# Heads in pairs: products on one half of the partitions next to those on the other half, in attention and in the stick-breaking mixer

## The chip, the cores and the metric

The kernel runs on 1 core of one Trainium2 chip. The metric is the device time of one execution in microseconds (us), as the median of several runs.

## The reference

The program is two transformer blocks in a row, on 256 positions of width 1024, all in float32. The change touches one mixer of each block. In the first block this is sliding-window attention with 16 query heads of 64 and 2 key heads, a window of 128 and a learned sink, for each block of 128 queries against its own and the previous 128 keys:

```
s = einsum('bqhgd,bkhd->bhgqk', qj, kj) * 64 ** -0.5        # where(band), else -inf
m = maximum(max(s, axis=-1), sink)
p = exp(s - m);  denom = sum(p, axis=-1) + exp(sink - m)
out = einsum('bhgqk,bkhd->bqhgd', p / denom, vj)
```

In the second block it is stick-breaking attention with 8 heads of 64, strictly causal (s < t), in two blocks of 128 queries:

```
z = einsum('bhtd,bhsd->bhts', q, k) * scale
sp = where(causal, softplus(z), 0);  rest = cumsum(sp, reverse=True) - sp
w = where(causal, exp(log_sigmoid(z) - rest), 0)
out = einsum('bhts,bhsd->bhtd', w, v)
```

Around them stand, in the first block, an mLSTM mixer, gates and output products and a PEER layer (a gather of 16 experts for each of 8 heads and each position); in the second block an HGRN2 mixer, gates, output products and a gated feed-forward layer.

## The kernel before, in words

The activations lie transposed (features on the partitions) as pairs of a high and a low float32r tile; the projections take three matmuls for each pair (L123, L126, L127). Their weights are streamed from memory in tiles of 128x1024 (`stream`, L112), copied by ScalarE (hi) and subtracted by VectorE or GpSimd (lo, L110).

The order in which each engine's instructions stand is not that of the source: a planner takes them by their place in the source and by when they would be ready in its own model of time. So projections that come later in the source fill the waits of the heads. `after(later, earlier)` (L96) ties two instructions in that order without a semaphore. In the second block the pieces of the mixers are laid between the projections by `weave` (L174) at the places `W_SB`, `W_HG` and so on (L28 to L31).

PSUM has eight banks: four of the tag "acc" (projections), two of "sm" and two of "s".

Attention (L473 to L519) runs over two blocks of queries (`tt`), two key heads (`g`) and two halves (`par_`). The transposed queries `qT` hold two heads in each 128 partitions, the even one on the partitions 0 to 63 and the odd one on 64 to 127, and `kT` holds each key head twice, on both halves. One unit of the loop (`tt`, `g`, `par_`) does four heads of one half: a mask is written into a bank of the tag "sm" by a matmul over all 128 partitions (L487), the scores of two or four heads are added to it by matmuls over 64 partitions (L491), VectorE takes the maximum (L494) and ScalarE the exponential (L499) into `pt_`, which has three buffers under the tag "s4"; then the sum and the sink (L502 to L505), the product with the reciprocal (L506), four transposes into a bank of the tag "s" (L510), a copy by ScalarE for the first block of keys and by VectorE for the second (L513, L515), and the product with the values, 64 columns of weights, into one half of the partitions of the bank `po` (L516). A group (`tt`, `g`) ends with the split of `po` into `attTh` and `attTl` (shown as aTh, aTl), which `mix_a` (L653, matmuls L123 to L127) reads.

Stick-breaking: `sb_z` (L940) writes for each of four heads a mask (L948) and the scores (L949, L950) into an "sm" bank, copies it (L951) and takes the minimum (L952); `sb_out` (L978) multiplies the weights with the values (L986, L987), two heads into the two halves of the partitions of one bank.

A float32 matmul is recorded in the profile as two MATMULs, each with its own load of weights.

Of the kernel before, what the change touches and what calls it, by code (L numbers as in the profile page):

```python
# [16 lines left out]
AF = mybir.ActivationFunctionType  # L17
ALU = mybir.AluOpType
# [29 lines left out]
def peer_hybrid_kernel(ctx: ExitStack, tc: tile.TileContext, A: dict, out: bass.AP, dbg=None, stop=None):  # L48
# [277 lines left out]
    with ExitStack() as c1:  # L326
# [146 lines left out]
        for tt in range(2):  # L473
            for g in range(2):
                po = bank("s")
                for par_ in range(2):
                    heads = [g * 8 + par_ + 2 * i for i in range(4)]
                    hs = slice(g * 8 + par_, g * 8 + par_ + 7, 2)
                    pr = slice(par_ * 64, par_ * 64 + 64)
                    W = P * (tt + 1)  # L480
                    per = 512 // W
                    pt_ = ten([P, 4, W], "pP", bufs=3, tag="s4")
                    nm = ten([P, 4], "nm", bufs=2)
                    sums = ten([P, 4], "sums", bufs=2)
                    for i0 in range(0, 4, per):
                        b = bank()
                        T.matmul(b, identb, (m_gt4.rearrange("p a b -> p (a b)") if tt == 0 else  # L487
                                             m_band.rearrange("p a c b -> p (a c b)")), start=True, stop=False)
                        for i in range(i0, i0 + per):
                            h = heads[i]  # L490
                            T.matmul(b[:, (i - i0) * W:(i - i0 + 1) * W], qT[pr, h // 2, tt * P:(tt + 1) * P],  # L491
                                     kT[pr, g, 0:W], start=False, stop=i == i0 + per - 1)
                        bv = b.rearrange("p (i s) -> p i s", i=per)
# [4 lines left out]
                        for i in range(i0, i0 + per):  # L498
                            S.activation(pt_[:, i], bv[:, i - i0], AF.Exp, bias=nm[:, i:i + 1],  # L499
                                         accum_out=sums[:, i:i + 1])  # L500
                    es = ten([P, 4], "es", bufs=2)
                    V.tensor_tensor(es, nm, par("sink")[:, hs], op=ALU.add)  # L502
                    S.activation(es, es, AF.Exp)
                    V.tensor_tensor(es, es, sums, op=ALU.add)
                    V.reciprocal(es, es)  # L505
                    V.tensor_tensor(pt_, pt_, bc(es.unsqueeze(2), [P, 4, W]), op=ALU.mult)  # L506
                    for sb in range(tt + 1):
                        b = bank("s")
                        for i in range(4):
                            T.transpose(b[:, i * P:(i + 1) * P], pt_[:, i, sb * P:(sb + 1) * P], ident)  # L510
                        pT = ten([P, 512], "pT", bufs=2)
                        if sb == 0:
                            S.activation(pT, b, AF.Copy)  # L513
                        else:
                            V.tensor_copy(pT, b)  # L515
                        T.matmul(po[pr, :], kv[:, sb, P + g * 64:P + g * 64 + 64], pT, start=sb == 0, stop=sb == tt)  # L516
# [319 lines left out]
    with ExitStack() as c4:  # L836
# [103 lines left out]
        def sb_z(g):  # L940
            zc = ten([P, 4, 384], "zc", bufs=2)
            l_ = ten([P, 4, 384], "sl", bufs=2)
            for i in range(4):
                h = g * 4 + i
                m, pr = h // 2, slice(h % 2 * 64, h % 2 * 64 + 64)
                z = bank()
                zz = z[:, 0:384]
                T.matmul(zz, identb, m_sb.rearrange("p a b -> p (a b)"), start=True, stop=False)  # L948
                T.matmul(z[:, 0:256], kT2[pr, m, 0:P], qT2[pr, m, :], start=False, stop=False)  # L949
                T.matmul(z[:, 256:384], kT2[pr, m, P:256], qT2[pr, m, P:256], start=False, stop=True)  # L950
                S.activation(zc[:, i], zz, AF.Copy)  # L951
                V.scalar_tensor_tensor(l_[:, i], zz, -1.0, zc[:, i], op0=ALU.mult, op1=ALU.min)  # L952
# [25 lines left out]
        def sb_out(g):  # L978
            zc = sb[g]["zc"]
            for m in range(g * 2, g * 2 + 2):  # L980
                ob = bank("s")
                for u in range(2):
                    h = m * 2 + u
# [252 lines left out]
```

## Time and profile before

| what | value |
|---|---|
| runs of the kernel | 1372.96, 1373.87, 1379.27 us; median 1373.87 |
| the profiled execution, its own time | 1372.99 us |
| its span, first to last instruction | 1371.2 us |
| busy: PE, DVE, ACT, POOL | 1202.5, 894.8, 514.4, 565.6 us |
| mean granted clock of TensorE | 0.951 |
| read from memory | 381.42 MB, 279 GB/s over the span |

The table is read so: PE is TensorE's matmuls, PEld its loads of weights, DVE VectorE, ACT ScalarE, POOL GpSimd. A busy share is a mean over stages of different kinds; the stages are, in order, the first block's mixers (to about 330 us), the gather of the experts (to about 960 us), and the second block.

### The profile page before, as it was taken

The page shows a single profiled execution, that of the slowest core. Times are in us where ns is not written, and L with a number is a line of the kernel's source. Part 1 is how long each engine was busy: PE and PEld are TensorE (multiplying, and loading weights), DVE is VectorE, ACT ScalarE, POOL GpSimd, SP SyncE. Part 2 cuts the span into 40 slices and gives each one's busy share as a digit, 9 for nine tenths or more (in the row PEclk, how much of TensorE's full clock was granted, in tenths as well). Part 3 has the DMA queues.
Part 4 walks back from the last instruction along what each step waited for, and adds up shares of the span by engine and source line. Part 5 has one row for each costly group of instructions (what it writes and reads, how often), then busy time and mean ns, then how long its engine had stood idle before and what let it go on. Part 6 is the DMA issues. An engine that isn't in the chain of part 4 may idle for free.

```text
span 1371.2 us, 16704 instructions
## 1 busy us (share of the span) xinstructions
PE 1202.5 (88%) x5785; PEld 832.8 (61%) x5785; DVE 894.8 (65%) x1963; ACT 514.4 (38%) x927; POOL 565.6 (41%) x394
## 2 busy tenths in 40 slices
PE   8999999994977778788877777887999999999998
PEld 7976789983333333333323333332788999899987
DVE  6966658558577776667877666765589786543521
ACT  6565434453122222212322221221475464544442
POOL 4311412542444435354444544443100005488874
PEclk9999999995899989899999999999999999999999
DMA  7533335666999999999999999999355335556554
GB/s 220 171 136 108 124 93 164 196 195 247 426 427 427 427 427 425 427 427 413 419 424 422 427 415 421 418 423 428 114 169 170 108 95 185 182 164 203 184 197 144
DMA packets 69779, 383.56 MB, mean 280 GB/s; under 512 B 8000, under 2 KB 8512, under 8 KB 36928
## 3 DMA queue, kind: packets, MB, share of 16 engines
q0 software_dynamic: 36864, 268.45, 46.7%
q1 hardware_dynamic: 31968, 112.15, 25.9%
q10 hardware_dynamic: 864, 1.90, 0.4%
q8 instruction: 46, 0.75, 0.2%
q14 instruction: 37, 0.30, 0.1%
HBM read 381.42 MB, written 1.05 MB: 279 GB/s over the span
## 4 chain that ended last, share of the span: by engine, by line
PE 44%; DMA 29%; DVE 17%; issue 4%; POOL 4%; ACT 1%; POOLq 0%; DVEq 0%; SPq 0%; ACTq 0%
DMA ga<-in_peer_du_dram,idx 28%; PE acc L123 10%; PE acc L126 10%; PE acc L127 10%; DVE jk L796 6%; POOL ga L793 3%; PE acc L805 2%; PE sm L126 1%; PE sm L123 1%; PE sm L127 1%; POOL lo L110 1%; PE sm L491 1%; DVE lo L110 1%; PE sm L1055 1%; PE s L516 1%
## 5 line engine op out<-in xcount | busy, mean ns | idle before, releaser
L805 PE MATMUL acc<-ga,dg 128*128 128x512 f32 x1024 | 497.9, 645 | 149.6 <-ACT dg L802 149.6
L805 PEld LDWEIGHTS acc<-ga,dg 128*128 128x128 f32 x1024 | 206.9, 207 | 439.5 <-issue 242.7
L793 POOL DMA_INDIRECT ga<-in_peer_du_dram,idx x256 | 292.1, 1141 | 356.0 <-PE acc L805 207.1
L796 DVE SCALAR_TENSOR_TENSOR jk<-ga,xn 128x1024 bf16<-128x1024 f32 x256 | 313.3, 1224 | 191.3 <-DMA ga<-in_peer_du_dram,idx 190.9
L110 POOL TENSOR_TENSOR lo<-raw,hi 128x1024 fp32r<-128x1024 f32 (+1 forms) x88 | 218.3, 2486 | 375.8 <-PE acc L127 243.6
L106 ACT ACTIVATE hi<-raw 128x1024 fp32r<-128x1024 f32 (+1 forms) x210 | 220.5, 1052 | 252.2 <-PE acc L127 54.6
L110 DVE TENSOR_TENSOR lo<-raw,hi 128x1024 fp32r<-128x1024 f32 (+1 forms) x122 | 163.1, 1338 | 94.0 <-ACT hi L106 36.2
L123 PE MATMUL acc<-T1l,hi 128*128 128x256 f32 x384 | 108.4, 283 | 0.3 <-DVE T1l L239 0.3
L126 PE MATMUL acc<-T1h,lo 128*128 128x256 f32 x384 | 108.4, 282 | 0.0
L127 PE MATMUL acc<-T1h,hi 128*128 128x256 f32 x384 | 107.8, 281 | 0.0
L123 PE MATMUL acc<-lo,T1h 128*128 128x512 f32 (+1 forms) x256 | 99.7, 395 | 2.2 <-DVE lo L110 2.0
L126 PE MATMUL acc<-hi,T1l 128*128 128x512 f32 (+1 forms) x256 | 100.2, 392 | 0.7 <-DVE T1l L308 0.6
L127 PE MATMUL acc<-hi,T1h 128*128 128x512 f32 (+1 forms) x256 | 99.9, 391 | 0.0
L123 PEld LDWEIGHTS acc<-T1l,hi 128*128 128x128 f32 x384 | 72.5, 189 | 1.9 <-issue 0.7
L127 PEld LDWEIGHTS acc<-T1h,hi 128*128 128x128 f32 x384 | 72.3, 188 | 0.9 <-issue 0.4
L126 PEld LDWEIGHTS acc<-T1h,lo 128*128 128x128 f32 x384 | 72.2, 188 | 1.0 <-issue 0.5
L126 PEld LDWEIGHTS acc<-hi,T1l 128*128 128x128 f32 x256 | 49.3, 192 | 12.0 <-DVE T1l L308 2.0
L123 PEld LDWEIGHTS acc<-lo,T1h 128*128 128x128 f32 x256 | 48.7, 192 | 11.5 <-DVE lo L110 2.2
L127 PEld LDWEIGHTS acc<-hi,T1h 128*128 128x128 f32 x256 | 49.1, 192 | 10.3 <-issue 1.0
L126 PE MATMUL sm<-fhTh,lo 128*128 128x256 f32 x176 | 48.5, 277 | 0.0
L127 PE MATMUL sm<-fhTh,hi 128*128 128x256 f32 x176 | 48.4, 276 | 0.0
L126 PE MATMUL acc<-fhTh,lo 128*128 128x256 f32 x176 | 48.4, 277 | 0.0
(849 smaller groups left out, 1984.2 us busy)
## 6 DMA issues: line engine op xcount, KB each, us to landing
raw<-in_w_in_dram SPq DMA_DIRECT2D x92, 512.0 KB, 3.5
raw<-in_w_fg_dram SPq DMA_DIRECT2D x22, 512.0 KB, 3.6
raw<-in_w_fu_dram SPq DMA_DIRECT2D x22, 512.0 KB, 3.8
raw<-in_w_fd_dram SPq DMA_DIRECT2D x22, 512.0 KB, 4.2
raw<-in_w_out_dram SPq DMA_DIRECT2D x16, 512.0 KB, 3.6
raw<-in_w_ba_dram SPq DMA_DIRECT2D x8, 512.0 KB, 3.5
raw<-in_w_bm_dram SPq DMA_DIRECT2D x8, 512.0 KB, 4.0
raw<-in_peer_wq_dram SPq DMA_DIRECT2D x8, 512.0 KB, 4.2
```

Of the source, the lines that this page charges most:

```text
L106: S.activation(dst_h, src, AF.Copy)
L110: return (V if eng == "v" else G).tensor_tensor(dst_l, src, dst_h.bitcast(F32), op=ALU.subtract)
L123: m = T.matmul(o, lh, rl, start=start, stop=False)
L126: T.matmul(o, ll, rh, start=False, stop=False)
L127: return T.matmul(o, lh, rh, start=False, stop=stop)
L491: T.matmul(b[:, (i - i0) * W:(i - i0 + 1) * W], qT[pr, h // 2, tt * P:(tt + 1) * P], kT[pr, g, 0:W], start=False, stop=i == i0 + per - 1)
L516: T.matmul(po[pr, :], kv[:, sb, P + g * 64:P + g * 64 + 64], pT, start=sb == 0, stop=sb == tt)
L793: G.indirect_dma_start(ga, None, A["peer_du"], bass.IndirectOffsetOnAxis(idx[tt][h][:, r0 + j:r0 + j + 1], 0))
L796: dot = V.scalar_tensor_tensor(jk, ga[:, 0:D], 1.0, xn[:, tt], op0=ALU.mult, op1=ALU.mult, accum_out=s_[:, j:j + 1])
L805: T.matmul(uacc[tt][dh], dg[:, j], rows[j][:, D + dh * 512:D + dh * 512 + 512], start=h + r0 + j == 0, stop=h == 7 and r0 + j == 15)
L1055: T.matmul(b[:, tt * 4 + m], xl_[:, m, tt], xr_[:, m, tt, :, 1], start=tt + m == 0, stop=tt + m == 4)
```

## The change

Attention: the two halves `par_` of a group are worked on together. For each group there are two score tiles, two sets of maxima and sums (four buffers each). The masks of both halves are written first, into the two "sm" banks; then the score matmuls of the halves alternate, head by head, and all are tied behind the second mask. The maxima and exponentials follow for the one half and then the other, and the sums, reciprocals and products likewise. For each block of keys both halves are transposed and copied, the first half's copy by ScalarE and the second's by VectorE (`pT` has three buffers), and then the two products with the values follow each other, the second half's first, tied behind the last transpose and to one another.

Stick-breaking: `sb_z` takes two heads at a time, with both masks first and the score matmuls alternating; `sb_out` alternates the products of its two heads.

```diff
@@ -473,47 +473,61 @@
         for tt in range(2):
             for g in range(2):
                 po = bank("s")
-                for par_ in range(2):
-                    heads = [g * 8 + par_ + 2 * i for i in range(4)]
-                    hs = slice(g * 8 + par_, g * 8 + par_ + 7, 2)
-                    pr = slice(par_ * 64, par_ * 64 + 64)
-                    W = P * (tt + 1)
-                    per = 512 // W
-                    pt_ = ten([P, 4, W], "pP", bufs=3, tag="s4")
-                    nm = ten([P, 4], "nm", bufs=2)
-                    sums = ten([P, 4], "sums", bufs=2)
-                    for i0 in range(0, 4, per):
-                        b = bank()
-                        T.matmul(b, identb, (m_gt4.rearrange("p a b -> p (a b)") if tt == 0 else
+                W = P * (tt + 1)
+                per = 512 // W
+
+
+                two_ = (0, 1)
+                pts = [ten([P, 4, W], "pP", bufs=3, tag="s4") for _ in two_]
+                nms = [ten([P, 4], "nm", bufs=4) for _ in two_]
+                sms = [ten([P, 4], "sums", bufs=4) for _ in two_]
+                for i0 in range(0, 4, per):
+                    bs = [bank() for _ in two_]
+                    for b in bs:
+                        mk = T.matmul(b, identb, (m_gt4.rearrange("p a b -> p (a b)") if tt == 0 else
                                              m_band.rearrange("p a c b -> p (a c b)")), start=True, stop=False)
-                        for i in range(i0, i0 + per):
-                            h = heads[i]
-                            T.matmul(b[:, (i - i0) * W:(i - i0 + 1) * W], qT[pr, h // 2, tt * P:(tt + 1) * P],
-                                     kT[pr, g, 0:W], start=False, stop=i == i0 + per - 1)
-                        bv = b.rearrange("p (i s) -> p i s", i=per)
+                    for i in range(i0, i0 + per):
+                        for par_ in two_:
+                            h = g * 8 + par_ + 2 * i
+                            pr = slice(par_ * 64, par_ * 64 + 64)
+                            after(T.matmul(bs[par_][:, (i - i0) * W:(i - i0 + 1) * W],
+                                           qT[pr, h // 2, tt * P:(tt + 1) * P], kT[pr, g, 0:W], start=False,
+                                           stop=i == i0 + per - 1), mk)
+                    for par_ in two_:
+                        nm = nms[par_]
+                        bv = bs[par_].rearrange("p (i s) -> p i s", i=per)
                         V.tensor_reduce(nm[:, i0:i0 + per], bv, axis=AX.X, op=ALU.max)
                         hsi = slice(g * 8 + par_ + 2 * i0, g * 8 + par_ + 2 * (i0 + per) - 1, 2)
                         V.scalar_tensor_tensor(nm[:, i0:i0 + per], nm[:, i0:i0 + per], -1.0, nsink[:, hsi],
                                                op0=ALU.mult, op1=ALU.min)
                         for i in range(i0, i0 + per):
-                            S.activation(pt_[:, i], bv[:, i - i0], AF.Exp, bias=nm[:, i:i + 1],
-                                         accum_out=sums[:, i:i + 1])
+                            S.activation(pts[par_][:, i], bv[:, i - i0], AF.Exp, bias=nm[:, i:i + 1],
+                                         accum_out=sms[par_][:, i:i + 1])
+                for par_ in two_:
+                    hs = slice(g * 8 + par_, g * 8 + par_ + 7, 2)
                     es = ten([P, 4], "es", bufs=2)
-                    V.tensor_tensor(es, nm, par("sink")[:, hs], op=ALU.add)
+                    V.tensor_tensor(es, nms[par_], par("sink")[:, hs], op=ALU.add)
                     S.activation(es, es, AF.Exp)
-                    V.tensor_tensor(es, es, sums, op=ALU.add)
+                    V.tensor_tensor(es, es, sms[par_], op=ALU.add)
                     V.reciprocal(es, es)
-                    V.tensor_tensor(pt_, pt_, bc(es.unsqueeze(2), [P, 4, W]), op=ALU.mult)
-                    for sb in range(tt + 1):
+                    V.tensor_tensor(pts[par_], pts[par_], bc(es.unsqueeze(2), [P, 4, W]), op=ALU.mult)
+                for sb in range(tt + 1):
+                    pTs = []
+                    for par_ in two_:
                         b = bank("s")
                         for i in range(4):
-                            T.transpose(b[:, i * P:(i + 1) * P], pt_[:, i, sb * P:(sb + 1) * P], ident)
-                        pT = ten([P, 512], "pT", bufs=2)
-                        if sb == 0:
+                            tr = T.transpose(b[:, i * P:(i + 1) * P], pts[par_][:, i, sb * P:(sb + 1) * P], ident)
+                        pT = ten([P, 512], "pT", bufs=3)
+                        if par_ == 0:
                             S.activation(pT, b, AF.Copy)
                         else:
                             V.tensor_copy(pT, b)
-                        T.matmul(po[pr, :], kv[:, sb, P + g * 64:P + g * 64 + 64], pT, start=sb == 0, stop=sb == tt)
+                        pTs.append(pT)
+                    for par_ in (1, 0):
+                        pv = T.matmul(po[par_ * 64:par_ * 64 + 64, :], kv[:, sb, P + g * 64:P + g * 64 + 64],
+                                      pTs[par_], start=sb == 0, stop=sb == tt)
+                        after(pv, tr)
+                        tr = pv
                 pv = po.rearrange("p (k t) -> p k t", k=4)
                 split(attTh[:, g * 4:g * 4 + 4, tt * P:(tt + 1) * P], attTl[:, g * 4:g * 4 + 4, tt * P:(tt + 1) * P],
                       pv, "v")
@@ -940,16 +954,19 @@
         def sb_z(g):
             zc = ten([P, 4, 384], "zc", bufs=2)
             l_ = ten([P, 4, 384], "sl", bufs=2)
-            for i in range(4):
-                h = g * 4 + i
-                m, pr = h // 2, slice(h % 2 * 64, h % 2 * 64 + 64)
-                z = bank()
-                zz = z[:, 0:384]
-                T.matmul(zz, identb, m_sb.rearrange("p a b -> p (a b)"), start=True, stop=False)
-                T.matmul(z[:, 0:256], kT2[pr, m, 0:P], qT2[pr, m, :], start=False, stop=False)
-                T.matmul(z[:, 256:384], kT2[pr, m, P:256], qT2[pr, m, P:256], start=False, stop=True)
-                S.activation(zc[:, i], zz, AF.Copy)
-                V.scalar_tensor_tensor(l_[:, i], zz, -1.0, zc[:, i], op0=ALU.mult, op1=ALU.min)
+            for i in range(0, 4, 2):
+                m = (g * 4 + i) // 2
+                zs = [bank()[:, 0:384] for _ in range(2)]
+                for zz in zs:
+                    mk = T.matmul(zz, identb, m_sb.rearrange("p a b -> p (a b)"), start=True, stop=False)
+                for s0 in range(2):
+                    for u, zz in enumerate(zs):
+                        pr = slice(u * 64, u * 64 + 64)
+                        after(T.matmul(zz[:, s0 * 256:384 if s0 else 256], kT2[pr, m, s0 * P:s0 * P + P],
+                                       qT2[pr, m, s0 * P:], start=False, stop=s0 == 1), mk)
+                for u, zz in enumerate(zs):
+                    S.activation(zc[:, i + u], zz, AF.Copy)
+                    V.scalar_tensor_tensor(l_[:, i + u], zz, -1.0, zc[:, i + u], op0=ALU.mult, op1=ALU.min)
             S.activation(l_, l_, AF.Exp)
             sb[g].update(zc=zc, l=l_)
 
@@ -979,12 +996,13 @@
             zc = sb[g]["zc"]
             for m in range(g * 2, g * 2 + 2):
                 ob = bank("s")
-                for u in range(2):
-                    h = m * 2 + u
-                    pr = slice(u * 64, u * 64 + 64)
-                    w_ = zc[:, h % 4]
-                    T.matmul(ob[pr, 0:256], vs[:, 0, h * 64:(h + 1) * 64], w_[:, 0:256], start=True, stop=False)
-                    T.matmul(ob[pr, P:256], vs[:, 1, h * 64:(h + 1) * 64], w_[:, 256:384], start=False, stop=True)
+                for s0 in range(2):
+                    for u in range(2):
+                        h = m * 2 + u
+                        pr = slice(u * 64, u * 64 + 64)
+                        w_ = zc[:, h % 4]
+                        T.matmul(ob[pr, s0 * P:256], vs[:, s0, h * 64:(h + 1) * 64], w_[:, s0 * 256:384 if s0 else 256],
+                                 start=s0 == 0, stop=s0 == 1)
                 split(oTh[:, m], oTl[:, m], ob[:, 0:256], "v")
```

## Rows read from the trace of the kernel before

**Rows 1.** The page, part 1: busy us (share of the span) and instructions of each engine.
```profile
PE 1202.5 (88%) x5785; PEld 832.8 (61%) x5785; DVE 894.8 (65%) x1963; ACT 514.4 (38%) x927; POOL 565.6 (41%) x394
```

**Rows 2.** Table by stretches: length; busy of PE, PEld, DVE, ACT, POOL; clock, DMA share, GB/s.
```profile
73.00:165.00 92.00, 90.61 (x439) 62.00 (x438) 60.83 (x94) 52.44 (x122) 24.59 (x10) 1.00 0.38 122
330.00:960.00 630.00, 486.62 (x1004) 202.58 (x1005) 427.08 (x1121) 138.90 (x383) 286.95 (x251) 0.91 1.01 423
1060.00:1130.00 70.00, 70.00 (x549) 65.11 (x549) 56.62 (x107) 39.77 (x48) 0.00 (x0) 1.00 0.32 105
```

**Rows 3.** Groups by line and shape, 73:165: count | busy, mean ns | idle before, releaser.
```profile
L516 PE MATMUL s<-pT,kv 128*64 128x512 f32 x24 | 12.9, 618 | 1.4 <-DVE pT L515 1.4
...
L491 PE MATMUL sm<-kT,qT 64*128 64x256 f32 x32 | 9.3, 405 | 0.0
...
L491 PE MATMUL sm<-kT,qT 64*128 64x128 f32 x32 | 4.6, 285 | 0.0
...
L499 ACT ACTIVATE pP<-sm,nm 128x256 f32<-128x256 f32 x16 | 7.4, 469 | 7.8 <-DVE nm L496 7.6
...
L515 DVE COPY pT<-s 128x512 f32<-128x512 f32 x4 | 2.7, 685 | 5.9 <-PE s L510 5.9
```

**Rows 4.** Timeline of PE, first block of queries: start, length, instruction, count.
```profile
72.89 0.40 PE L123 MATMUL acc<-lo,T1h 128*128 128x512 f32 x1
73.13 0.39 PE L487 MATMUL sm<-m_gt,identb 128*128 128x512 bf16 x1
73.45 1.16 PE L491 MATMUL sm<-kT,qT 64*128 64x128 f32 x8
74.54 0.39 PE L487 MATMUL sm<-m_gt,identb 128*128 128x512 bf16 x1
```

**Rows 5.** Timeline of PE, second block of queries.
```profile
90.62 0.39 PE L487 MATMUL sm<-m_band,identb 128*128 128x512 bf16 x1
90.94 1.13 PE L491 MATMUL sm<-kT,qT 64*128 64x256 f32 x4
92.00 0.50 PE L126 MATMUL acc<-hi,T1l 128*128 128x512 f32 x1
```

**Rows 6.** Timeline of PE, one product with the values.
```profile
88.57 0.39 PE L127 MATMUL acc<-hi,T1h 128*128 128x512 f32 x1
88.89 1.07 PE L516 MATMUL s<-pT,kv 128*64 128x512 f32 x2
89.89 0.66 PE L510 MATMUL s<-cst,pP 128*128 128x128 f32 x4
```

**Rows 7.** Timeline of PE, one head of the stick-breaking scores.
```profile
1075.93 0.34 PE L948 MATMUL sm<-m_sb,identb 128*128 128x384 bf16 x1
1076.20 0.70 PE L949 MATMUL sm<-qT,kT 64*128 64x256 f32 x2
1076.74 0.38 PE L950 MATMUL sm<-qT,kT 64*128 64x128 f32 x2
1077.05 0.38 PE L123 MATMUL acc<-T1l,hi 128*128 128x256 f32 x1
```

**Rows 8.** Timeline of PE, one pair of heads of the stick-breaking output.
```profile
1105.59 0.66 PE L986 MATMUL s<-zc,vs 128*64 128x256 f32 x4
1106.07 0.39 PE L987 MATMUL s<-zc,vs 128*64 128x128 f32 x4
1106.29 0.65 PE L986 MATMUL s<-zc,vs 128*64 128x256 f32 x4
```

**Rows 9.** L714 by stretches: length; busy of PE, PEld (records touched); clock, DMA share, GB/s.
```profile
311.88:312.23 0.35, 0.35 (x4) 0.35 (x4) 1.00 0.33 129
312.23:312.58 0.35, 0.35 (x9) 0.35 (x8) 1.00 1.47 129
```

**Rows 10.** Instructions on the tile aTh: count, ns (least, median, most), first and last start.
```profile
L126 PE MATMUL acc<-aTh,lo x64: 276/276/366, 187.9 to 214.6; 128*128 128x256 f32 x64
...
L106 ACT ACTIVATE aTh<-s x4: 587/597/597, 97.4 to 163.9; 128x512 fp32r<-128x512 f32 x4
```

## The prediction

> **What bounds the kernel now.** I read the page's busy shares first. The reader is to see that no engine is at work all the time and that TensorE has the largest share [rows 1]; that is an average over stages, so the table by stretches comes next. The middle stage, 330 to 960 us, is the expert gather: DMA share 1.01, 423 GB/s, PE 486.62 of 630 us [rows 2]. It holds none of the edited lines, and a faster TensorE gives nothing there. The edited lines lie elsewhere: attention at 73 to 165 us, with PE at work for 90.61 of 92 us against DVE 60.83 and ACT 52.44, and stick-breaking at 1060 to 1130 us, with PE at work for 70.00 of 70 us; the granted clock is 1.00 in both, the upper level (2.4 GHz), so no slower clock is there to be cured [rows 2]. In these two stages TensorE is the bound, projections fill every wait of the heads, and what comes off its queue comes off the span, unless a new wait replaces it. The groups of lines by shape show that the only PE idle time in front of an edited line is 1.4 us, before one L516 [rows 3].
>
> How much comes off is read from the starts in the timeline, not from mean durations: a product of f32 is recorded as two MATMULs (L491 has 64 records for 32 products [rows 3]), records overlap, and their ends are modelled. The distance from one block's start to the next block's start is what the queue pays.
>
> **Part 1, scores of attention (L487, L491).** First block of queries: the step between ordinary matmuls of 512 columns is 0.24 us (72.89 to 73.13); a mask takes 0.32 (73.13 to 73.45), four heads on one half of the partitions take 1.09 (73.45 to 74.54) [rows 4]. One unit is 1.41, two are 2.82. Afterwards both masks stand first (0.24 + 0.32), then four heads of one half next to four of the other. If the halves run side by side these take 1.09 together: 1.65. Saved 1.17, twice (g = 0, 1): 2.3 us. Second block: 0.32 + 1.06 = 1.38 a unit [rows 5]; two are 2.76, afterwards 0.24 + 0.32 + 1.06 = 1.62. Saved 1.14, four times: 4.6 us.
>
> Does the trace show halves side by side? For halves of the contraction there is one spot, the routing scores of L714, where four heads of the upper half are followed by four of the lower: in equal stretches of 0.35 us, 4 records are in flight with one half alone, and 9 where one half gives way to the other, at the same clock [rows 9]. For halves of the output columns there is L986/L987, below. So I take full overlap; the other end is none at all.
>
> **Part 2, products with the values (L516).** Entering costs 0.32 against 0.24 (88.57 to 88.89), the product 1.00 (88.89 to 89.89) [rows 6]. There are 12 (24 records [rows 3]), each by itself with transposes or projections behind it; afterwards 6 pairs, the second of a pair on the other 64 columns. Each pair saves 1.00 + 0.08 = 1.08: 6.5 us.
>
> **Part 3, stick-breaking scores (L948 to L950).** Mask 0.27, scores 0.85, 1.12 a head (1075.93 to 1077.05) [rows 7]. Two heads 2.24; afterwards a mask of 384 columns behind ordinary work (three quarters of 0.24: 0.18), one of 0.27, and 0.85 for both: 1.30. Saved 0.94, four times: 3.8 us.
>
> **Part 4, stick-breaking output (L986, L987).** The source lists head 0's two products, then head 1's. Yet four records of L986 start within one run of 0.66 us, and two heads are through after 0.70 us (1105.59 to 1106.29) [rows 8], where one head's products of the same column counts took 0.85 in part 3. They run in pairs already; alternating them in the source gives 0. Bounds: 0.2 us gained; if the new order broke the pairing, two heads would pay 2 x 0.85 and the four pairs lose 4.0. I take 0, since the new order makes neighbours of just those that overlap now.
>
> On this the Trainium skill speaks against the row: "TensorE: Matmul & The Clock Gate", in the section on packing small matmuls, says matmuls start and end strictly in queue order. Were that so and the queue in source order, head 1 could not start beside head 0, and part 4 would bring some 4 us by itself. The trace has them overlapping, so I go by the row.
>
> **What it adds.** Copies of the transposed weights now go to ACT for one half and to DVE for the other: 6 on each, where DVE had 4 [rows 3]. Its four gave the one wait of 1.4 us, 0.35 each; two more cost 0.7. A pair holds both buffers of the PSUM tag "sm" until its exponentials are through; queued behind such a wait are PE's projections, which the planner can put in front instead, as it does now (for one bank at a time). Without this cover PE stands until the pair's four exponentials of 0.47 us [rows 3] are through, 1.9 in each of the four pairs of the second block, 7.5 us; with it nothing. I take 0.5, near the covered end, since the same planner left 1.4 us idle in 92. A pair also takes two of the three buffers of "s4" at once (last rival). DVE's and ACT's instructions are otherwise the same in number and shape. No DMA is moved.
>
> **Sum.** 2.3 + 4.6 + 6.5 + 3.8 = 17.2 us less, 0.7 + 0.5 more: 16.0. The profiled execution took 1372.99 us (span 1371.2), 0.9 below the median of the runs, 1373.87. From the median: 1357.9, so 1358.
>
> **The rivals.**
> *Overlap in order only (0.12).* If a pass can start beside its predecessor in the queue but not past it, a pair of L516, two passes each, overlaps only in its middle: it saves one pass of four, 0.5 in place of 1.08, 3.5 less over six; the alternating scores end one pass late, 0.11 to 0.22 in ten pairs, 1.6 less. 16.0 - 5.1 = 10.9: 1363. Against it: rows 8 again. (The rule of the Trainium skill's TensorE page quoted under part 4 would make this of the pairs.)
> *Half the gain turned into waits (0.20).* PE comes earlier to its meeting points with DVE and ACT, and the 7.5 us of held banks are not covered: 16.0 - 7.0 = 9.0 in the middle of a spread of 4 to 12: 1365. For it: those waits for PE are what DVE and ACT are free for now. Against: 1.4 us idle in the whole stretch.
> *The halves do not run side by side (0.07).* Then only entries are saved: 0.08 for ten masks and six L516, 1.3 us, less than the 1.2 added: 1374. Against: rows 8 and 9.
> *Attention becomes too late (0.08), the slow side.* Its results are first read at 187.9 us (L126 on aTh); its four groups end between 97.4 and 163.9 [rows 10]. With 13.4 us saved ahead of it (parts 1 and 2), that reader comes at 174.5. Before, three buffers of "s4" served three units; now two go at once, so that the next group gets its second only when the last one's first is transposed. At worst that is 1.5 times the time per group: 73.1 + 1.5 x 90.8 = 209.3, 21.4 later than the present need, and PE, out of projections (the weights arrive in the source's order), stands. Less 3.8 from stick-breaking: +18, 1392. It costs from a stretch of 1.12 (174.5) on, and the kernel is slower than before from 1.31 (191.7). Against it: DVE and ACT are idle for a third of the stretch and more, and the groups' length now is mostly queueing behind projections.
>
> **How the numbers follow.** Forecast 0.53, rivals as given. A change under 0.5% (6.9 us) cannot be told from none: faster is below 1367.0, slower above 1380.7. Faster: 0.53 + 0.12 + two thirds of 0.20 = 0.78; slower 0.08; the same 0.14. The range, 1352 to 1370, takes in the forecast with the 1.4 us wait gone, part 4 at its better end and the runs' own spread of some microseconds, the ordered overlap, and nearly all of the half-lost case; outside lie the last two rivals and tails, about 0.18.
>
> **What would show it.** Right: blocks of 16 score records (first block of queries) in 1.1 us and of 8 (second block) in 1.1, four records of the value products in 1.0 to 1.1, stick-breaking pairs in 0.9; PE idle still under 3 us up to 165; the first read of aTh near 174; the gather stage as long as before, 13 us earlier. Ordered overlap: value pairs in 1.5. Half lost: PE idle before masks or L516 of 5 us or more, released by ACT or DVE. Too late: PE idle released by aTh. The prediction is wrong if the score blocks shrink and the span does not.

## The result, and the profile after

The changed kernel takes 1358.84 us in the median of four runs (1357.29 to 1364.63), the kernel before 1376.57 in the four runs beside it (1372.96 to 1380.8). The ratio of the runs is 0.989, with a 95% interval of 0.9862 to 0.9918: faster by 0.8 to 1.4%. The forecast was 1358 us, with a range of 1352 to 1370. The profiled execution took 1357.29 us (span 1355.5), 15.7 less than that of before (1372.99).

The page of the changed kernel, its span and its part 1, against [rows 1]: the count of TensorE's instructions is the same, and its busy time is 11.4 us shorter.

```profile
span 1355.5 us, 16706 instructions
...
PE 1191.1 (88%) x5785; PEld 828.1 (61%) x5785; DVE 889.3 (66%) x1965; ACT 511.8 (38%) x925; POOL 564.8 (42%) x394
```

Where the time went is read from four marks, each the first or last start of a group that is in both kernels: the first mask of attention (L487), the first routing score, the last expert product, the first feed-forward product. They are the tables of the tiles m_gt, keys, dg and fhTl (count, ns least/median/most, first and last start). Of the kernel before:

```profile
L487 PE MATMUL sm<-m_gt,identb x4: 379/390/390, 73.1 to 83.6; 128*128 128x512 bf16 x4
...
L714 PE MATMUL sm<-keys,qqT x64: 272/417/579, 311.7 to 322.3; 64*128 64x128 f32 x64
...
L805 PE MATMUL acc<-ga,dg x1024: 592/592/1222, 339.9 to 971.9; 128*128 128x512 f32 x171
...
L123 PE MATMUL acc<-fhTl,hi x176: 276/276/282, 1181.9 to 1301.0; 128*128 128x256 f32 x176
```

Of the changed kernel:

```profile
L487 PE MATMUL sm<-m_gt,identb x4: 389/390/390, 73.1 to 85.3; 128*128 128x512 bf16 x4
...
L728 PE MATMUL sm<-keys,qqT x64: 272/395/579, 299.1 to 309.6; 64*128 64x128 f32 x64
...
L819 PE MATMUL acc<-ga,dg x1024: 592/592/1222, 327.4 to 957.2; 128*128 128x512 f32 x171
...
L123 PE MATMUL acc<-fhTl,hi x176: 276/276/282, 1163.3 to 1285.5; 128*128 128x256 f32 x176
```

The differences of these starts, and the same for every experiment below (us):

| kernel | mask to routing | routing to last expert product | to first feed-forward product | to the end of the span |
|---|---|---|---|---|
| before | 238.6 | 660.2 | 210.0 | 189.3 |
| changed | 226.0 | 658.1 | 206.1 | 192.2 |
| changed_again | 226.0 | 658.0 | 205.9 | 191.8 |
| e1_attention_only | 227.3 | 657.2 | 209.6 | 194.3 |
| e2_sb_scores_only | 239.5 | 658.7 | 207.6 | 192.8 |
| e3_sb_out_only | 238.8 | 661.1 | 211.4 | 191.4 |
| e4_same_half | 230.5 | 659.5 | 209.1 | 190.1 |
| e5_values_apart | 230.1 | 658.4 | 206.1 | 190.7 |
| e6_half_after_half | 228.3 | 658.9 | 205.9 | 192.8 |
| e7_four_buffers | 226.4 | 658.7 | 205.9 | 191.0 |
| e8_more_pairs | 226.1 | 657.8 | 206.3 | 190.6 |
| e9_mlstm_tied | 223.8 | 657.3 | 206.1 | 191.3 |
| e10_tied_and_later_spread | 224.3 | 657.7 | 206.1 | 191.0 |
| e10_again | 224.2 | 658.3 | 205.9 | 186.8 |

The reader is to see: 12.6 us come from the stretch with attention, 3.9 from the one with stick-breaking. The gather stage, which no edit but one of e8 touches, lies between 657.2 and 661.1 in the fourteen profiles. Its 2.1 us here cannot be told from scatter; but the three kernels with the old attention average 660.0 and the other eleven profiles 658.2, and why is open. The last stretch gives 2.9 back, which is looked at below. The first and third columns repeat within 0.2 us for the same program (changed and changed_again, e10 and e10_again), which is why they, and not single times, carry the experiments; between programs they can also differ by TensorE's clock and pace, as e1 and e2 show.

The timeline of PE in the changed kernel (start, length, instruction, count). Scores of attention, first and second block of queries, against [rows 4, 5]:

```profile
73.57 0.39 PE L487 MATMUL sm<-m_gt,identb 128*128 128x512 bf16 x1
73.89 1.16 PE L493 MATMUL sm<-kT,qT 64*128 64x128 f32 x16
74.98 0.50 PE L127 MATMUL acc<-hi,T1h 128*128 128x512 f32 x1
...
106.04 0.39 PE L487 MATMUL sm<-m_band,identb 128*128 128x512 bf16 x1
106.36 1.14 PE L493 MATMUL sm<-kT,qT 64*128 64x256 f32 x8
107.42 0.50 PE L123 MATMUL acc<-lo,T1h 128*128 128x512 f32 x1
```

Sixteen records take 1.09 us (73.89 to 74.98), as eight did before; eight of 256 columns take 1.06, as four did. The products with the values, against [rows 6]:

```profile
94.66 1.08 PE L527 MATMUL s<-pT,kv 128*64 128x512 f32 x4
95.67 0.49 PE L123 MATMUL acc<-lo,T1h 128*128 128x512 f32 x1
...
124.52 1.07 PE L527 MATMUL s<-pT,kv 128*64 128x512 f32 x2
125.53 0.39 PE L487 MATMUL sm<-m_band,identb 128*128 128x512 bf16 x1
125.57 0.47 PE L123 MATMUL acc<-T1l,hi 128*128 128x256 f32 x1
125.96 1.07 PE L527 MATMUL s<-pT,kv 128*64 128x512 f32 x2
126.97 0.44 PE L519 MATMUL s<-cst,pP 128*128 128x128 f32 x2
```

Four records in 1.01 us (94.66 to 95.67) instead of two in 1.00. But at 124.52 the planner laid a mask and a projection between the two products, and that pair took 1.01 twice. It is the one of six; one score pair, at 96.32, is cut in the same way. Stick-breaking, against [rows 7, 8]:

```profile
1060.07 0.34 PE L961 MATMUL sm<-m_sb,identb 128*128 128x384 bf16 x1
1060.34 0.92 PE L965 MATMUL sm<-qT,kT 64*128 64x256 f32 x8
1061.19 0.38 PE L123 MATMUL acc<-T1l,hi 128*128 128x256 f32 x1
...
1087.81 1.52 PE L1004 MATMUL s<-zc,vs 128*64 128x256 f32 x16
1089.26 0.39 PE L127 MATMUL acc<-T1h,hi 128*128 128x256 f32 x1
```

Two heads' scores take 0.85 (1060.34 to 1061.19), as one did. The output of four heads takes 1.45 (1087.81 to 1089.26), where 1.50 were needed before (1105.59 to 1107.09): hardly anything to gain there, as forecast.

What TensorE waited for, in the groups by line and shape of 73:165, against [rows 3], and the table by stretches, against [rows 2]:

```profile
L527 PE MATMUL s<-pT,kv 128*64 128x512 f32 x24 | 7.5, 618 | 0.0
L519 PE MATMUL s<-cst,pP 128*128 128x128 f32 x48 | 7.4, 278 | 2.4 <-DVE pP L513 2.4
```

```profile
73.00:165.00 92.00, 88.66 (x532) 67.89 (x531) 60.35 (x102) 56.67 (x128) 24.77 (x11) 1.00 0.44 142
330.00:960.00 630.00, 501.40 (x1042) 208.57 (x1041) 425.44 (x1115) 140.51 (x388) 287.47 (x252) 0.92 0.99 416
1040.00:1110.00 70.00, 70.00 (x575) 65.95 (x574) 57.77 (x111) 41.61 (x51) 0.00 (x0) 1.00 0.36 114
```

The wait of L516 for VectorE's copy is gone (now L527, 0.0), and one of 2.4 us stands before a transpose instead. In the 92 us TensorE now gets through 532 records where it was 439: the place of the second half's products was taken by later projections.

### The profile page after: what moved, and what is told of

Same layout as the page of the kernel before. It is cut to its first block, busy times and chain, and to the rows that moved or that the text cites. A ratio compares the mean times of both kernels' runs of the same rounds, so it can differ in the third digit from the quotient of the medians.

```text
span 1355.5 us, 16706 instructions
## 1 busy us (share of the span) xinstructions
PE 1191.1 (88%) x5785; PEld 828.1 (61%) x5785; DVE 889.3 (66%) x1965; ACT 511.8 (38%) x925; POOL 564.8 (42%) x394
## 4 chain that ended last, share of the span: by engine, by line
PE 43%; DMA 26%; DVE 16%; POOL 6%; issue 6%; ACT 2%; POOLq 0%; ACTq 0%; DVEq 0%
DMA ga<-in_peer_du_dram,idx 24%; PE acc L123 10%; PE acc L126 10%; PE acc L127 10%; POOL ga L807 5%; DVE jk L810 5%; PE acc L819 3%; DVE lo L110 1%; POOL lo L110 1%; PE sm L126 1%; PE sm L127 1%; PE sm L123 1%; PE sm L1073 1%; ACT hi L106 1%; DMA raw<-in_w_fg_dram 1%
## 5 line engine op out<-in xcount | busy, mean ns | idle before, releaser
L819 PEld LDWEIGHTS acc<-ga,dg 128*128 128x128 f32 x1024 | 207.6, 207 | 436.8 <-issue 245.7
L807 POOL DMA_INDIRECT ga<-in_peer_du_dram,idx x256 | 295.9, 1156 | 354.0 <-PE acc L819 233.3
L810 DVE SCALAR_TENSOR_TENSOR jk<-ga,xn 128x1024 bf16<-128x1024 f32 x256 | 313.1, 1223 | 190.9 <-DMA ga<-in_peer_du_dram,idx 190.6
L110 DVE TENSOR_TENSOR lo<-raw,hi 128x1024 fp32r<-128x1024 f32 (+1 forms) x122 | 166.1, 1363 | 112.4 <-ACT hi L106 38.9
L123 PE MATMUL sm<-fhTl,hi 128*128 128x256 f32 x176 | 49.2, 284 | 0.0
```

The lines of the kernel that those rows point to most:

```text
L110: return (V if eng == "v" else G).tensor_tensor(dst_l, src, dst_h.bitcast(F32), op=ALU.subtract)
L123: m = T.matmul(o, lh, rl, start=start, stop=False)
L807: G.indirect_dma_start(ga, None, A["peer_du"], bass.IndirectOffsetOnAxis(idx[tt][h][:, r0 + j:r0 + j + 1], 0))
L810: dot = V.scalar_tensor_tensor(jk, ga[:, 0:D], 1.0, xn[:, tt], op0=ALU.mult, op1=ALU.mult, accum_out=s_[:, j:j + 1])
L819: T.matmul(uacc[tt][dh], dg[:, j], rows[j][:, D + dh * 512:D + dh * 512 + 512], start=h + r0 + j == 0, stop=h == 7 and r0 + j == 15)
```

## The experiments

The theory is that of the prediction: the halves run side by side on TensorE, and as TensorE bounds both stages the saving passes on. Its rivals: the gain is the planner's new order or the fewer entries; products overlap only with their neighbour in the queue; the new waits take part of it.

**One part at a time.** e1 has the changed attention with the old `sb_z` and `sb_out`:

```
-            for i in range(0, 4, 2):
+            for i in range(4):
...
```

> Only the attention part of the change; stick-breaking as before. If TensorE's saving passes through stage by stage, the routing scores begin near 299.1 us as in the changed kernel (before: 311.7), and the stretch from the last expert product to the feed-forward's first product is as long as before, 3.5 us longer than in the changed kernel: near 1362 us. If the saving of one part depends on the other, the start of the routing scores moves away from 299.

The profiled execution took 1364.92 us. Mask to routing is 227.3, close to the changed kernel's 226.0, and the stick-breaking stretch 209.6, like before. The routing scores began at 302.0 and not 299.1: 1.6 us were lost ahead of the first mask, at the start of the program (the first mask stands at 74.7), and 1.3 behind it. The main reason for these 1.3 is the clock. The table by stretches, PE alone, from the end of the wait of 2.4 us on, in the changed kernel:

```profile
144.20:152.04 7.84, 7.84 (x69) 1.00 0.40 133
```

and for the same 69 records in e1:

```profile
145.80:155.42 9.62, 9.62 (x69) 0.82 0.33 120
```

The granted clock fell to 1.2 GHz in e1 (0.50 from 148 to 150 us), and the records took 1.8 us more. A later wait of 1.0 us (L587) was gone for it, and 0.5 came to it at the end of the stretch. So the two parts add up. But the new wait can have a price that the two profiles of the changed kernel do not show. In eight profiles it lasted 2.2 to 2.5 us; behind it the clock fell in six of them (e1, e6, e8, e9 and both of e10), and not in the two of the changed kernel. In the other six profiles the longest wait in attention was 1.1 to 1.5 us, and the clock stayed at 1.00 up to the routing scores. What decides among the eight is open.

e2 has the old kernel with the new `sb_z` alone:

```
-            for i in range(4):
+            for i in range(0, 4, 2):
...
```

> Only the stick-breaking scores in pairs. If each pair saves 0.94 us, the routing scores begin at 311.7 as before and the stretch from the last expert product to the feed-forward's first product is 3.5 to 3.8 us shorter than before: 1370. If the gain of that stage came from elsewhere, nothing moves: 1374.

1375.31 us, where 1370 was expected. The stick-breaking stretch is 207.6, 2.4 shorter than before; the four pairs stand in it with 0.85 us each as in the changed kernel. It is 1.5 longer than there, so the expected 3.5 were not reached; the ordinary products beside the pairs ran at the slower of two paces in this execution (last section). The routing scores begin 2.7 later than before: 1.8 ahead of the first mask, where TensorE waited 2.3 us for VectorE (L465), and 0.9 in the first stretch. This run shows the pairs, and also that one time on the clock cannot show 3 us here. e3 has only the new order of the output:

```
-                for u in range(2):
-                    h = m * 2 + u
+                for s0 in range(2):
+                    for u in range(2):
...
```

> Only the order of the stick-breaking output products is changed. If the two heads ran side by side already, the time is that of the kernel before, 1374 within 2 us, and a pair of heads takes 0.70 us as before. If TensorE started products strictly in the source's order, the four pairs would now bring 4 us: 1370.

1377.12 us; four heads take 1.45 us in place of 1.50, 0.1 in all. The stretch is 211.4, longer than before (210.0), as ordinary products ran at the slower pace here too. The output's order brings next to nothing.

**Overlap taken away, order kept.** e4:

```
-                            pr = slice(par_ * 64, par_ * 64 + 64)
+                            pr = slice(0, 64)
...
-                        pr = slice(u * 64, u * 64 + 64)
+                        pr = slice(0, 64)
```

> The changed kernel with both heads of a pair read from the partitions 0 to 63 in the score products of attention and stick-breaking (so the odd heads compute with the even heads' queries and keys); the order of TensorE's instructions is the same, nothing can run side by side in the scores. If running side by side is what saves, the score blocks double: attention 2 x 0.9 + 4 x 0.86 = 5.2 us, so the routing scores begin near 304.3, stick-breaking 4 x 0.65 = 2.6 more: about 1366.6 us. If the new order and the fewer entries make the gain, nothing changes: 1358.8.

1363.99 us. Mask to routing 230.5 (4.5 more than changed), stick-breaking 209.1 (3.0 more); expected were 5.2 and 2.6, and nothing by the rival. The timeline of PE in e4:

```profile
73.78 2.05 PE L493 MATMUL sm<-kT,qT 64*128 64x128 f32 x16
75.75 0.50 PE L127 MATMUL acc<-hi,T1h 128*128 128x512 f32 x1
...
1066.52 1.57 PE L965 MATMUL sm<-qT,kT 64*128 64x256 f32 x8
1068.02 0.38 PE L123 MATMUL acc<-T1l,hi 128*128 128x256 f32 x1
```

The same sixteen records, in the same place of the same queue, take 1.97 us in place of 1.09, and the eight of stick-breaking 1.50 in place of 0.85. The groups of records start in the same order in both kernels, from the first to the last. That settles it for the scores: most of what is saved is due to the operands' lying on different halves of the partitions. Summed over all starts, the score blocks of attention take 12.99 us before, 11.84 in e4 and 7.06 in the changed kernel, those of stick-breaking 6.78, 6.00 and 3.42. So the rival has a share: 1.2 and 0.8 us come with the order and the fewer entries, which e4 keeps, and 4.8 and 2.6 from the halves.

**The values' products apart.** e5:

```
-                        pTs.append(pT)
-                    for par_ in (1, 0):
-                        pv = T.matmul(po[par_ * 64:par_ * 64 + 64, :], ...
+                        T.matmul(po[par_ * 64:par_ * 64 + 64, :], ..., pT, start=sb == 0, stop=sb == tt)
```

> The changed kernel, with each half's product with the values right behind its own copy again, so that no two stand side by side. If pairing them saves 1.08 us six times, the routing scores begin 6.5 us later, near 305.5, and the time is 1365. If the pair's saving is lost in waiting for the later of the two copies, they begin near 299 and the time stays at 1359.

1362.06 us. Mask to routing is 230.1, 4.1 more than changed, not 6.5: the prediction's size of this term was too large. In the groups by line and shape of e5 the 24 records are as busy as in [rows 3]:

```profile
L524 PE MATMUL s<-pT,kv 128*64 128x512 f32 x24 | 12.9, 618 | 1.1 <-DVE pT L523 1.1
```

The starts in the timeline say why it is not 6.5: these records take 12.0 us in e5 as before and 7.1 in the changed kernel, where one pair of six is cut; that is 5.0. In e5, in turn, no score pair is cut, which is worth 0.6. TensorE also waited 2.0 us less in e5 (3.2 between the marks, against 5.1), and its other products took 1.7 longer. So 5.0 is what the pairs save in the queue, and the 4.1 holds waits and scatter as well.

**The order within a pair.** e6 lists all products of one half and then all of the other:

```
-                    for i in range(i0, i0 + per):
-                        for par_ in two_:
+                    for par_ in two_:
+                        for i in range(i0, i0 + per):
...
```

> The changed kernel with the score products of the one half all ahead of those of the other, instead of alternating. If TensorE lets a product of the free half start past some of its predecessors (about four records, as in the routing scores), only the blocks of 16 records lose, 0.5 us twice, and the others 0.1 each: 1360 to 1361, routing scores near 300.5. If products overlap only with their neighbour in the queue, nearly all of the scores' overlap goes, 5.2 us in attention and 2.6 in stick-breaking: 1366.

The timeline of PE in e6:

```profile
74.23 1.71 PE L493 MATMUL sm<-kT,qT 64*128 64x128 f32 x16
75.87 0.50 PE L127 MATMUL acc<-hi,T1h 128*128 128x512 f32 x1
...
1063.67 0.93 PE L967 MATMUL sm<-qT,kT 64*128 64x256 f32 x8
1064.53 0.38 PE L123 MATMUL acc<-T1l,hi 128*128 128x256 f32 x1
```

1361.52 us. Sixteen records take 1.64 us: between 1.09 (alternating) and 1.97 (no overlap). Four behind four take 0.86, the same as alternating. The single starts show the reach: the first record of the second half starts at 74.785 us, beside the fifth of the first half (74.780), when three of that half still wait. In the routing scores of the kernel before it is the same (312.241 beside the fifth at 312.235). So TensorE starts products of the free half past three waiting records of the busy one; an alternating order is needed only for longer rows. The stick-breaking stretch is unchanged (205.9), mask to routing 2.3 longer: 1.4 more in the score blocks (8.5 against 7.1 us, summed over all starts; transposes cut the second of the two long ones), 1.0 less in the values' products, none of which is cut here, and 1.8 more around other products, where the clock fell (139 to 142.5 us). The Trainium skill's page "TensorE: Matmul & The Clock Gate", in its section on packing small matmuls, has matmuls start in strict order of the queue; the measurement differs, and it decides.

**The wait for normalised scores.** e7:

```
-                pts = [ten([P, 4, W], "pP", bufs=3, tag="s4") for _ in two_]
+                pts = [ten([P, 4, W], "pP", bufs=4, tag="s4") for _ in two_]
...
```

> The changed kernel with four buffers of the tag s4 instead of three. If the 2.4 us for which TensorE waited on the normalised scores come from the pair's hold on two of three buffers, they go and the routing scores begin near 297: 1356.5. If they are a matter of the queue behind VectorE, nothing changes: 299, 1359.

1357.02 us. Neither: mask to routing is 226.4 against 226.0. The wait of L519 fell from 2.4 to 1.1 us, but one of 1.5 for the copies of L524 took its place. The hold on buffers costs nothing on balance.

**More pairs.** The mLSTM scores (L623, L624) and the routing scores were still one half at a time. e8:

```
+            for pair in {0: ((0, 1), (2, 3)), 3: ((4, 5),), 6: ((6, 7),)}[h0]:
...
+                bs_ = [bank() for _ in pair]
+                prev_ = None
+                for s0 in range(2):
+                    for u, b in enumerate(bs_):
...
+                        sc_ = T.matmul(b[:, s0 * 256:384 if s0 else 256], mkT[pr, m, s0 * P:s0 * P + P],
+                                       mqT[pr, m, s0 * P:], start=s0 == 0, stop=s0 == 1)
+                        if prev_ is not None:
+                            after(sc_, prev_)
+                        prev_ = sc_
...
```

> The changed kernel, with the mLSTM scores and the routing scores in pairs of halves as well. If the same saving holds, four mLSTM pairs bring 4 x 0.85 = 3.4 us ahead of the routing scores, which begin near 295.7, and the gather starts about 1 us sooner still: 1354 to 1355. If that stage is held by VectorE's chain of the gates and the normalisation instead, the start stays at 299: 1358.

1357.45 us (six runs, 1355.86 to 1359.39), 0.988 of before, 0.9859 to 0.9902: no gain to be seen over the change, and mask to routing is 226.1. The routing pairs bring nothing: from the first routing score to the first expert product it is 28.2 us, against 28.3 in the changed kernel. The timeline of PE in e8 shows the reason for the mLSTM's part:

```profile
158.58 0.70 PE L629 MATMUL sm<-mqT,mkT 64*128 64x256 f32 x2
159.21 0.38 PE L126 MATMUL acc<-T1h,lo 128*128 128x256 f32 x1
...
165.72 0.92 PE L629 MATMUL sm<-mqT,mkT 64*128 64x256 f32 x6
166.56 0.38 PE L123 MATMUL acc<-aTl,hi 128*128 128x256 f32 x1
```

The planner let the first product go 7 us ahead, as its own bank was free, so it ran alone, and a pair takes 0.63 + 0.84 us where two heads took 2 x 0.85. Four such pairs save 0.9 us, less than the 1.8 that a fall of the clock cost in e1, and in this execution it fell too (145 to 149 us). In the changed kernel no score can go before the mask in the second bank: that tie is a working part of it. e9 drops the routing pairs and puts a tie into the mLSTM's:

```
+                prev_ = T.matmul(bs_[1][:, 0:8], identb, identb[:, 0:8], start=True, stop=True)
...
+                        after(sc_, prev_)
+                        prev_ = sc_
```

> The changed kernel once more, as the measure for the next two: 1358 to 1359, the routing scores begin near 299 to 301.

> The changed kernel with the mLSTM scores in pairs, the first product tied behind a matmul of 8 columns that writes into the second head's bank, so that no product can start before both banks are free. In the run with more pairs the first product had been placed alone, and only 0.22 us of each pair was saved. If the missing tie was the reason, the mLSTM blocks shrink from 8 x 0.85 = 6.8 to 4 x 0.85 = 3.4 us, less some 0.2 for each small matmul: 2.6 us, about 1356. If that stretch is held by VectorE, the blocks shrink and the time does not: 1358 to 1359.

```profile
164.92 0.92 PE L629 MATMUL sm<-mqT,mkT 64*128 64x256 f32 x8
165.77 0.38 PE L126 MATMUL acc<-aTh,lo 128*128 128x256 f32 x1
```

Now all four pairs take 0.85 us (this row is of e9), mask to routing is 223.8, 2.2 shorter although the clock fell in it, and the time is 1354.88 us (five runs): 0.9843 of before, 0.9824 to 0.9863. The change itself, on the same chip, took 1360.91 (0.9891, 0.9873 to 0.9909). So e9 beats both kernels; the intervals do not meet. The medians lie 6.0 us apart and the profiled executions 2.1: mask to routing accounts for the 2.1, the rest is not explained.

**The wait ahead of the feed-forward layer.** e10 is e9 with this:

```
-                weave([proj_feat_steps(A["w_fg"], n, hTh, hTl, KD, ev_gate)], [(3, n4.spread)] if n == 0 else [])
-                proj_feat(A["w_fu"], n, hTh, hTl, KD, ev_up, tag="sm")
+                gs = proj_feat_steps(A["w_fg"], n, hTh, hTl, KD, ev_gate)
+                us = proj_feat_steps(A["w_fu"], n, hTh, hTl, KD, ev_up, tag="sm")
+                if n == 0:
+                    for _ in range(3):
+                        next(gs)
+                    for _ in range(2):
+                        next(us)
+                    n4.spread("s")
...
```

> As the run before, and ahead of the feed-forward layer the matmuls that spread the norm's factor over the rows (L263) stand behind two weight tiles of the up projection, in a bank of the tag s. If TensorE's wait of 3.2 us for VectorE there and the slower clock that follows it in most profiles (1.2 to 2.6 us) are removed, it is 4 to 5 us faster than the run before: 1351 to 1352. If the wait only moves to the next meeting point (the gate's evacuation), it is the same as the run before.

1352.92 us (five runs, 1352.35 to 1357.35), 0.9838 of before, 0.9817 to 0.986: not to be told from e9. TensorE's wait fell from 3.2 to 1.5 us and the clock stayed up behind it, but in the profiled execution the layer's products then ran slower, and the last stretch was as long as ever (191.0).

> The run before once more, for one look at the feed-forward layer, where its products of 256 columns started every 117.8 ns instead of 113.3 ns in the changed kernel. If that pace belongs to the kernel, it is 117.8 again and the layer ends as late; if it belongs to the execution, it can be 113.3, and the span is 3 to 4 us shorter, near 1349.

1350.55 us; the last stretch 186.8, 4.2 shorter, with the same program. The expectation that it depends on the execution and not on the kernel is the one that held. This execution was on another chip, which the last section comes back to.

## Why the prediction was right

**The bound.** TensorE was at work through both stages, and what left its queue left the span: 12.6 and 3.9 us in the two stretches, 16.5 together, against 12.2 (13.4 less 1.2) and 3.8 forecast. e4 shows the cause for the scores, e5 for the values. Summed over all starts between the marks of attention, the same instructions took 13.4 us less of TensorE's queue, just what parts 1 and 2 had forecast. That it fits so closely is luck: the terms were off in both directions and cancel.

**Part 1** (6.9 forecast): the score blocks lost 5.9 us (13.0 to 7.1, summed over all starts). That is the six pairs at their full size less 0.6 for the one that was cut. The forecast had 0.5 more for the entries of masks; the steps behind the twelve masks fell by 1.7, though part of that can belong to the projections next to them. **Part 2** (6.5): 5.0, the mis-sized term; the prediction took all six pairs as neighbours in the queue, and nothing but the order was tied, so that other products could come between. All remaining products of the stretch took 0.8 less. **Part 3** (3.8): 3.9 in the stretch; 4.0 in the scores and masks. **Part 4** (0): 0.1, e3.

**What it adds** (1.2): between the first mask and the routing scores TensorE waited for 5.2 us, where it was 4.4 before: 0.8. The size was about right in this execution and the place wrong: no product with the values waited for VectorE's copies, but one transpose for the normalised scores. e7 shows that buffers are not its price. Two things were not foreseen: e1, with the same attention, waited 4.2, so the 0.8 is uncertain by as much; and the wait can bring a fall of the clock, 1.8 us in e1.

**The rivals.** Overlap in order only: refuted by e6, and by the value pairs, which took 1.01 us and not 1.5. No overlap: refuted by e4. Half lost: not so, as no mask and no product with the values waited; but up to 165 us TensorE was idle for 3.3 us, a little more than the 3 that the prediction gave as its sign. Too late: the first read of aTh came at 161.2, not near 174, since the planner took the first of those products before the last group was done (its last aTh is written from 163.1 on), and no wait on aTh appears.

**The total.** It fits to 1 us, in part by chance. The four runs of the kernel before have a median of 1376.57, while the forecast was counted from 1373.87: the medians differ by 17.7 us, the profiled executions by 15.7, and 16.0 was forecast. Two things that were not forecast nearly cancel in the profiles: the gather stage (2.1 shorter) and the last stretch (2.9 longer). The latter begins with TensorE's wait of 3.2 us before L263, which both kernels have. The table by stretches of the changed kernel, over the wait and the products behind it:

```profile
1172.50:1185.80 13.30, 10.09 (x67) 9.92 (x66) 7.10 (x17) 5.25 (x7) 4.85 (x3) 0.74 0.41 120
```

and of the kernel before, over the same instructions:

```profile
1191.10:1201.80 10.70, 7.48 (x66) 7.32 (x65) 7.11 (x17) 5.27 (x8) 4.34 (x3) 1.00 0.43 149
```

The granted clock is 0.74 against 1.00: it stood at 1.2 GHz for part of the stretch after the wait, and the same work took 13.3 us in place of 10.7. Of the twelve profiles with that wait it fell at that place in nine, among them e3 with attention as before, and not in those of before, e2 and e6, the last of which has attention in pairs. So no edit is needed for it, and none brings it for certain. But it fell in eight of nine with attention in pairs and in one of three without, and whether the edits make it likelier is open.

## What to carry to other kernels

Two products that use 64 of the 128 partitions or 64 output columns cost one if they lie on different halves and stand near each other in TensorE's queue: look for lone products of that shape in a stage that TensorE bounds, and read the gain from the distance of starts, not from durations. Let no instruction come between the two: write into the second one's bank first and tie the first product behind that write, as e8 and e9 show. Look at the granted clock behind every new wait before a gain or a loss of 1 or 2 us is put down to an edit (e1, e8). And check in the timeline first whether the queue has paired them already, as it had in the stick-breaking output.

## What the runs showed of the hardware

TensorE takes products of the free half past three waiting records of the other (e6: 1.64 us for eight behind eight, against 1.09 and 1.97; the ninth record starts beside the fifth). The two column halves may write one PSUM bank at once (L527: four records in 1.01 us).

Long trains of the same products run at one of two paces, at a granted clock of 1.00. The table by stretches over 50 us of the feed-forward layer, PE alone (length, busy (records), clock, DMA share, GB/s), of e10:

```profile
1210.00:1260.00 50.00, 50.00 (x426) 1.00 0.61 182
```

and of e10_again, the same program:

```profile
1210.00:1260.00 50.00, 50.00 (x443) 1.00 0.60 189
```

426 records against 443, 4% apart: products start every 117.8 ns in the one execution and every 113.3 ns in the other, for the whole layer. It makes 4 us of the span and may be much of the scatter between runs. The two executions ran on different chips, but e1 to e8 ran on one, and there the products of this layer started every 117.8 ns in e1, e2 and e6 and every 113.3 in the others; so the chip alone does not choose the pace, and what does stays open.
